# Hybrid block on one core: value transposes issued behind the inversion's recursion, gate projections ahead of query and key projections, long GpSimd operations cut in four

## The chip, the cores and the metric

The kernel runs on one core of a Trainium2 chip. The metric is the device time of one execution in microseconds (us), taken as the median of several. A core has five engines that work side by side and meet through semaphores: TensorE (PE in the profile, with PEld for its weight loads) does matmuls, VectorE (DVE) and ScalarE (ACT) do elementwise work, GpSimd (POOL) does elementwise work from on-chip memory to on-chip memory, and SyncE (SP) issues DMA transfers. [...]

## The reference

One encoder layer on 512 tokens of width 1024, all in float32. A single projection of the normalised input feeds a bidirectional RWKV-7 recurrence (8 heads of 64), a 2D neighbourhood attention (8 heads of 64) and 2048 gate logits. Both results are gated and projected back, and a mixture of experts follows (32 experts, two per token).

```python
h = rmsnorm(x, norm1_g)
p = h @ w_in
p_rwkv, q, k, v, gate_logits = jnp.split(p, IN_SPLITS, axis=-1)
y_a = rwkv7_bidirectional(p_rwkv, ...) @ w_o_rwkv
y_b = neighbourhood_attention_2d(q, k, v, q_gain, k_gain, rpb) @ w_o_na
g_a, g_b = jnp.split(jax.nn.sigmoid(gate_logits + b_gate), 2, axis=-1)
x = x + (g_a * y_a + g_b * y_b) @ w_out
x = x + hierarchical_moe(rmsnorm(x, norm2_g), ...)
```

The recurrence is, for each direction, head and token: `sa = S @ (-kk)`, then `S = S * w + outer(sa, kk * a) + outer(v, k)`, then `y = S @ r`. Inside the attention, q and k are normalised per head (a mean of squares, a reciprocal root, a gain) before they are used; v and the gates are not.

## The kernel before

Features lie on the 128 partitions and tokens along the free axis, so one "column block" of the projection is a tile of 128 x 512. A column block costs 24 matmuls 128x512, since each float32 product is made of three (high and low parts of the weights `w_hi`, `w_lo` and of the input `hT_hi`, `hT_lo`). ACT makes `w_hi`, and DVE or, for the late blocks, POOL makes `w_lo` (POOL in four parts of 128x256).

The recurrence is computed in chunks of 32 tokens, 16 chunks (`NCH`), for two groups of four heads (g = 0 and 1; a group has two column blocks q of two heads each). Each group goes through four stages:

- `prep(g)`: shifted inputs `sh_k`, `sh_r`, `sh_v`, the decays (`s`, `ep`), the scaled keys `KB`, and per chunk the matrices `T` (products `tp<-T,KB` on PE, masked by DVE into `T` or copied by ACT into `MT`).
- `invert(g)` (line 584): a triangular 32x32 matrix per chunk is inverted. DVE transposes `MT` into `NT`, runs a recursion of 15 steps on 16x16 halves (each one product `pr<-NT,TI` and one sum `TI<-TI,pr`, each depending on the last), and transposes the result twice (`MT<-TI`, `NT<-TI`, lines 609 and 611). Then PE multiplies by the off-diagonal part, once per direction d: `c<-MT,O`, ACT copies to `Q`, `c<-Q,NT`, and DVE adds to `MT`.
- `v_chunks(q)` (line 570): 16 DVE transposes 32x512 per group put the values into the state tile `R`. The first chain step reads them. `bonus_pair` (line 557) then makes `bv` on DVE and writes it to memory.
- `chain(g)` (chain_step, line 635): 16 steps, one after the other. A step is PE `c<-R,T`, ACT `X<-c`, PE `c<-X,MT`, ACT and DVE copies `R<-c`, PE `c<-R,T`, and two DVE sums `R<-c,EX` that start the next step. `chain_out` normalises the result.

PE has more to do beside this: `others(n)` (line 766) projects the next n of 28 further column blocks at a low priority, so that their matmuls fill PE's gaps. Block m = 0 to 3 is q, 4 to 7 is k (both end in `na_qk`, line 783), 8 to 11 is v (`na_v`), 12 to 27 are the gates. `na_qk` needs two ACT passes, eight small matmuls `x<-cst,osq` for the head sums, nine DVE operations on 128x8 (`ngx`, `nrs_i`, `nst`: a reciprocal root by Newton steps), a DVE copy `osq<-nst`, four matmuls `x<-cst,osq` 128x128, and the DVE products `oth<-oth,qg,x` (q) or `oth<-oth,pv,x` (k). A gate block needs one ACT tanh. All results are stored to memory and are read back by the attention (`na_inputs`, one half of the heads at a time) or by the gating. The blocks are taken 3, 5, 8 and 2 at a time (`OTH`), around `prep(0)`, `chain(0)` and `prep(1)`; then one after each of the eight attention blocks, which run beside `chain(1)`; then the rest.

The order of each engine's queue is fixed when the program is built: a list scheduler places instructions by priority as their operands come ready in its own model. So a change of source order or of priorities moves instructions on all engines.

Setting up at the start, `rwkv_consts` (lines 355 to 371) lets POOL copy identity blocks into the whole of `T` (four copies of 64x2048) and clear parts of `R` (four of 32x2048). In `prep_unit`, for the second direction, POOL adds the keys of both directions (`kd<-kd,kd`, 128x512, line 478), which `bonus_pair` reads.

After the attention follow the gating and output projection, the routing, and the experts, whose weights are streamed from memory.

## Time and profile before

| | us |
|---|---|
| median of three executions | 918.54 |
| lowest and highest of them | 910.8 and 920.9 |
| the profiled execution | 916.96 |
| its span, first to last instruction | 915.2 |

The profiled execution is read in these stages (us from the start of the span, as the first and last instructions of a stage stand in the timeline): set-up and first projections 0 to 40, prep 0 from 40 to 124.5, recursion 0 to 136.2, products of inversion 0 and first chain step to 166, chain 0 to about 264 with prep 1 begun beside it, prep 1 to 348.8, recursion 1 to 359.7, products and first chain step to 384, chain 1 and the attention to 513, remaining projections to 551, then gating, routing and experts to 915.

A row of a table by stretches gives start and end, the length, then the busy microseconds of PE, PEld, DVE, ACT and POOL (number of instructions in brackets), the granted TensorE clock as a share of full speed, the DMA share and GB/s. A row of a timeline gives start, length, engine, line, operation, result<-inputs, shapes, and in square brackets how long the engine had been idle and what ended that. A row of a table by groups ends with the count, the busy time in total, the mean of one in ns, and the idle time before them.

### The profile page before, as it was taken

How to read it: one execution, taken by the hardware profiler on the slowest of the kernel's cores; microseconds unless marked ns; L12 is line 12 of the kernel's file. 1: busy time of each engine (PE TensorE's matmuls, PEld its weight loads, DVE VectorE, ACT ScalarE, POOL GpSimd, SP SyncE). 2: the span in 40 equal slices, each digit the busy share in tenths (PEclk: the TensorE clock that was granted, in tenths of full speed). 3: DMA queues.
4: the chain of work that ended last, by engine and by line, in shares of the span. 5: the costliest groups of instructions: out<-in, count | busy, mean ns of one | idle time of the engine just before them, and what ended most of it. 6: DMA issues, size and time to landing. Idle time of an engine off the chain costs nothing. (4 is left out here: it accounts for less than half of the span.)

```text
span 915.2 us, 17391 instructions
## 1 busy us (share of the span) xinstructions
PE 809.7 (88%) x7192; PEld 526.2 (57%) x7192; DVE 419.5 (46%) x870; ACT 309.4 (34%) x667; POOL 199.4 (22%) x248
## 2 busy tenths in 40 slices
PE   8999886989988987799998999999579999888884
PEld 7776655656667665566666677878433333333331
DVE  5699883565788677124346205643612111111010
ACT  6544521222444553126647522223211111111110
POOL 2611231120004243132313430003411212211010
PEclk9999995999999998699999999999779999999998
DMA  6320130221112322321314648889889999999982
GB/s 220 114 73 33 36 103 27 70 72 66 46 62 87 101 70 71 131 91 44 116 45 138 189 134 317 300 316 401 343 358 411 389 362 398 394 394 399 399 339 44
DMA packets 49263, 176.18 MB, mean 193 GB/s; under 512 B 7584, under 2 KB 14368, under 8 KB 37152
## 3 DMA queue, kind: packets, MB, share of 16 engines
q1 hardware_dynamic: 43936, 164.56, 48.9%
q0 software_dynamic: 5248, 10.50, 4.3%
q8 instruction: 57, 0.93, 0.4%
q14 instruction: 22, 0.18, 0.1%
HBM read 159.30 MB, written 24.12 MB: 200 GB/s over the span
## 5 line engine op out<-in xcount | busy, mean ns | idle before, releaser
L191 POOL TENSOR_TENSOR w_lo<-w_raw,w_hi 128x256 fp32r<-128x256 f32 x116 | 88.7, 796 | 225.0 <-ACT w_hi L188 225.0
L203 PE MATMUL G<-ws,xT 128*64 128x512 f32 x512 | 128.8, 600 | 4.1 <-DMA ws<-in_wgu 2.8
L203 PE MATMUL mm<-hT_hi,w_lo 128*128 128x512 f32 x264 | 113.0, 428 | 8.4 <-ACT oth L188 7.6
L203 PE MATMUL mm<-hT_hi,w_hi 128*128 128x512 f32 x264 | 111.4, 422 | 0.0
L203 PE MATMUL mm<-hT_lo,w_hi 128*128 128x512 f32 x264 | 110.8, 420 | 0.0
L203 PEld LDWEIGHTS G<-ws,xT 128*64 128x64 f32 x512 | 44.5, 138 | 76.6 <-issue 65.4
L203 PE MATMUL Yd<-ws,hT 128*64 128x512 f32 x256 | 65.7, 606 | 9.7 <-ACT y L188 8.6
L188 ACT ACTIVATE w_hi<-w_raw 128x1024 fp32r<-128x1024 f32 x59 | 62.3, 1055 | 31.2 <-PE mm L203 31.2
L203 PEld LDWEIGHTS mm<-hT_hi,w_lo 128*128 128x128 f32 x264 | 51.4, 195 | 26.0 <-issue 15.5
L191 DVE TENSOR_TENSOR w_lo<-w_raw,w_hi 128x1024 fp32r<-128x1024 f32 x30 | 39.3, 1308 | 50.2 <-ACT w_hi L188 50.2
L203 PEld LDWEIGHTS mm<-hT_lo,w_hi 128*128 128x128 f32 x264 | 51.5, 195 | 12.7 <-issue 2.2
L203 PEld LDWEIGHTS mm<-hT_hi,w_hi 128*128 128x128 f32 x264 | 51.8, 196 | 11.3 <-issue 1.5
L1386 POOL DMA_INDIRECT out<-y,idx x16 | 25.2, 1577 | 117.1 <-DVE y L198 100.4
L191 DVE TENSOR_TENSOR sg<-sg,G 128x256 f32<-128x256 f32 x16 | 6.7, 420 | 95.9 <-ACT sg L188 95.9
L188 ACT ACTIVATE sg<-G,wts 128x256 f32<-128x256 f32 x16 | 7.6, 474 | 116.9 <-PE G L203 116.9
L198 DVE TENSOR_SCALAR y<-Yd,wts 128x512 f32<-128x512 f32 (+1 forms) x16 | 11.7, 734 | 77.1 <-PE Yd L203 62.6
L655 DVE COPY R<-c 32x128 f32<-32x128 f32 x64 | 18.8, 293 | 52.1 <-ACT R L188 51.4
L203 PEld LDWEIGHTS Yd<-ws,hT 128*64 128x64 f32 x256 | 16.6, 136 | 43.5 <-ACT y L188 21.6
L203 PE MATMUL c<-R,T 128*32 128x64 f32 (+1 forms) x992 | 36.5, 231 | 3.6 <-DVE R L191 1.3
L203 PE MATMUL tp<-T,KB 64*64 64x128 f32 x512 | 34.5, 278 | 5.6 <-ACT T L188 5.3
L203 PEld LDWEIGHTS c<-R,T 128*32 128x32 f32 (+1 forms) x992 | 26.2, 125 | 22.6 <-issue 10.5
L188 ACT ACTIVATE T<-tp 64x256 f32<-64x256 f32 x64 | 23.9, 378 | 42.8 <-DVE T L191 41.8
(313 smaller groups left out, 1454.3 us busy)
## 6 DMA issues: line engine op xcount, KB each, us to landing
ws<-in_wgu SPq DMA_DIRECT2D x64, 1024.0 KB, 21.0
ws<-in_wd SPq DMA_DIRECT2D x30, 1024.0 KB, 22.2
w_raw<-in_w_in SPq DMA_DIRECT2D x43, 512.0 KB, 3.6
d_oth<-oth SPq DMA_DIRECT2D x16, 256.0 KB, 3.1
w_raw<-in_wo SPq DMA_DIRECT2D x8, 512.0 KB, 3.8
w_raw<-in_w_out SPq DMA_DIRECT2D x8, 512.0 KB, 5.1
x_in<-in_x SPq DMA_DIRECT2D x4, 512.0 KB
ga<-d_oth SPq DMA_DIRECT2D x8, 256.0 KB, 4.5
```

Source lines behind the costliest of these rows:

```text
L188: self.nc.scalar.activation(out, in_, func, **kw)
L191: (eng or self.nc.vector).tensor_tensor(out, a, b, op=op)
L198: self.nc.vector.tensor_scalar(out, a, s1, None, op0=op0)
L203: return self.nc.tensor.matmul(out, l, r, start=start, stop=stop, **kw)
L655: self.nc.vector.tensor_copy(R[u, :, blk, p2], ps[u, 2:4])
L1386: self.nc.gpsimd.indirect_dma_start(out=self.A["out"], out_offset=bass.IndirectOffsetOnAxis(ap=idx, axis=0), in_=y, in_offset=None, bounds ...
```

## The change

Three things are changed.

1. The order in which `others` takes its blocks. It was 0, 1, 2, ... 27. It is now `TURN`: eight gates (12 to 19), then 0, 1, 4, 5, 8, 9, 2, 3, then 10, 11, then 6, 7 and 20 to 25 at the attention blocks, and 26, 27.
2. `v_chunks` may be issued only behind the last transpose of `invert` (`issue_after` holds the instructions of its body back until that one is issued; it isn't a wait on the chip).
3. Three kinds of POOL operations are made of four parts each: the copies into `T` (64x2048 to 64x512), the clearing of `R` (32x2048 to 32x512), and the sum `kd` (128x512 to 128x128).

```diff
+TURN = list(range(12, 20)) + [0, 1, 4, 5, 8, 9, 2, 3, 10, 11, 6, 7] + list(range(20, 28))
...
-                nc.gpsimd.tensor_copy(self.T[sr, :, d, blk, :, 64:], id64[sr, None, None].to_broadcast([64, NCH, 2, 64]))
+                for n in range(0, NCH, 4):
+                    nc.gpsimd.tensor_copy(self.T[sr, n:n + 4, d, blk, :, 64:], id64[sr, None, None].to_broadcast([64, 4, 2, 64]))
...
-            nc.gpsimd.memset(self.R[o:o + 32, :, :, blk, p2], 0.0)
+            for n in range(0, NCH, 4):
+                nc.gpsimd.memset(self.R[o:o + 32, n:n + 4, :, blk, p2], 0.0)
...
-            self.tt(self.kd[q], self.kd[q], kd, OP.add, eng=nc.gpsimd)
+            for o in range(0, T, P):
+                self.tt(self.kd[q][:, o:o + P], self.kd[q][:, o:o + P], kd[:, o:o + P], OP.add, eng=nc.gpsimd)
...
-        self.invert(g)
-        for q in (q0, q1):
-            self.v_chunks(q)
+        last = self.invert(g)
+
+        with self.tc.issue_after(last.ins):
+            for q in (q0, q1):
+                self.v_chunks(q)
         self.bonus_pair(q1)
...
-        nc.vector.transpose(out=D.rearrange("p u t -> p t u"), in_=TI.rearrange("p a b -> p b a"))
+        last = nc.vector.transpose(out=D.rearrange("p u t -> p t u"), in_=TI.rearrange("p a b -> p b a"))
...
             m = MT[:, d * NCH:(d + 1) * NCH]
             self.tt(m, m, ps, OP.add)
+        return last
...
-        for m in range(self.done, min(self.done + n, 28)):
+        for m in TURN[self.done:self.done + n]:
             ps = self.proj(15 + m, LOW)
```

In what follows, lines of the new kernel are 3 to 9 higher than those of the old (the transposes of the values are L581 before and L589 now). First, VectorE's queue at the end of recursion 0 and the start of chain 0. Before, it reads:

```order
L191 TENSOR_TENSOR TI<-TI,pr 128x2x15
L609 STREAM_TRANSPOSE MT<-TI 128x32x32
L194 SCALAR_TENSOR_TENSOR oth<-oth,qg,x 128x128 x4
L611 STREAM_TRANSPOSE NT<-TI 128x32x32
L191 TENSOR_TENSOR MT<-MT,c_1405 128x512
L191 TENSOR_TENSOR bv<-sh_v_989,tp 128x512
L191 TENSOR_TENSOR MT<-MT,c_1538 128x512
L200 TENSOR_SCALAR ngx<-x 128x8
L689 TENSOR_SCALAR nrs_i<-ngx 128x8
L200 TENSOR_SCALAR nst<-nrs_i 128x8
L191 TENSOR_TENSOR nrs_i<-nst 128x8
```

The same place now:

```order
L194 TENSOR_TENSOR TI<-TI,pr 128x2x15
L617 STREAM_TRANSPOSE MT<-TI 128x32x32
L619 STREAM_TRANSPOSE NT<-TI 128x32x32
L589 STREAM_TRANSPOSE R<-sh_v_473 32x16x32 x7
L194 TENSOR_TENSOR MT<-MT,c_1336 128x512
L589 STREAM_TRANSPOSE R<-sh_v_473 32x16x32
L589 STREAM_TRANSPOSE R<-sh_v_1019 32x16x32 x5
L194 TENSOR_TENSOR MT<-MT,c_1469 128x512
L589 STREAM_TRANSPOSE R<-sh_v_1019 32x16x32 x3
L194 TENSOR_TENSOR bv<-sh_v_1019,tp 128x512
L664 COPY R<-c_2470 32x2x64 x2
L194 TENSOR_TENSOR R<-c_2470,EX 64x2x128 x2
```

Thirteen of the sixteen value transposes now stand ahead of the second sum into `MT` and three behind it, with `bv` behind these and ahead of the first step's copies; the query's normalisation (`ngx`, `nrs_i`, `nst`) that stood ahead of the first step's copies is gone. Around inversion 1 the rows are the same as these.

Second, VectorE's queue in prep 1, where the second direction's keys are masked. Before:

```order
L191 TENSOR_TENSOR T<-tp,cst_107 64x4x64
L191 TENSOR_TENSOR T<-sh_r_2110,ep 64x16x32
L191 TENSOR_TENSOR kd<-kd,sh_k_2075 128x512
L194 SCALAR_TENSOR_TENSOR a<-a,kk 128x512
L191 TENSOR_TENSOR KB<-kd,s 128x16x32
L191 TENSOR_TENSOR KB<-a,s 128x16x32
L191 TENSOR_TENSOR T<-tp,cst_107 64x4x64 x2
L194 SCALAR_TENSOR_TENSOR T<-sh_k_2075,nkk,ep 64x16x31
```

The same place now:

```order
L197 SCALAR_TENSOR_TENSOR a<-a,kk 128x512
L194 TENSOR_TENSOR KB<-kd,s 128x16x32
L203 TENSOR_SCALAR ngx<-x 128x8
L194 TENSOR_TENSOR KB<-a,s 128x16x32
L698 TENSOR_SCALAR nrs_i<-ngx 128x8
L194 TENSOR_TENSOR T<-tp,cst_107 64x4x64
L203 TENSOR_SCALAR nst<-nrs_i 128x8
L194 TENSOR_TENSOR T<-tp,cst_107 64x4x64
L194 TENSOR_TENSOR nrs_i<-nst 128x8
L197 SCALAR_TENSOR_TENSOR T<-sh_k_1853,nkk,ep 64x16x31
```

The normalisations of blocks 0, 1 and 4 now stand between the operations of prep 1; that of block 5 stands in the same way between the 30 operations of recursion 1, those of 2 and 3 in chain 1 (steps 2 and 3), and those of 6 and 7 later in chain 1, between attention blocks. Before, block 0 stood in prep 0, block 1 in recursion 0, and blocks 2 to 7 in chain 0.

Third, TensorE's queue at the products of inversion 0 and the first chain step. Before:

```order
L203 MATMUL c_1471<-MT,O 32x32 x41
L203 MATMUL c_2516<-R,T 32x64 x8
L203 MATMUL mm<-hT_hi,w_lo 128x512
L203 MATMUL mm<-hT_hi,w_hi 128x512
L203 MATMUL c_1538<-Q,NT 32x32 x64
L203 MATMUL c_2516<-X,MT 32x64 x4
```

Now:

```order
L206 MATMUL mm<-hT_hi,w_lo 128x512
L206 MATMUL c_1469<-Q,NT 32x32 x64
L206 MATMUL c_2470<-R,T 32x64 x4
L206 MATMUL mm<-hT_hi,w_hi 128x512
L206 MATMUL mm<-hT_lo,w_hi 128x512
```

The first step's `c<-R,T`, which reads the transposed values, stood ahead of the last product `c<-Q,NT`; it now stands behind it, in two halves (the first is shown) with nine matmuls of a gate projection between them.

## The prediction

> **What bounds the kernel now.** I read the spans first, then the busy time of the engines over the whole, then by stretches, then the timelines of the engines inside the stretches that the change touches.

> ```profile
> core 0: 915.2 us, clock 0.956
> DMA  6320130221112322321314648889889999999982
> ```

> The profiled execution has 915.2 us between its first and last instruction and 1.8 around it (916.96). Each digit of the second row is a fortieth of the span, 22.9 us: memory traffic is light until about 550 us and then near full until the end. What the change touches lies before that. Whatever it saves or costs there shifts the loaded part as a whole, at full value.

> ```profile
> 40.00:124.50 84.50, 78.86 (x715) 54.82 (x714) 74.96 (x130) 41.92 (x79) 16.40 (x20) 0.96 0.19 57
> 124.50:136.20 11.70, 8.50 (x42) 6.40 (x41) 10.44 (x45) 2.50 (x4) 3.11 (x4) 1.00 0.33 112
> 140.00:160.00 20.00, 14.12 (x419) 11.24 (x420) 5.78 (x12) 3.35 (x7) 2.79 (x4) 0.54 0.08 29
> 166.00:221.00 55.00, 49.54 (x590) 33.57 (x590) 31.55 (x100) 17.75 (x43) 8.43 (x12) 0.99 0.17 59
> 300.00:348.80 48.80, 44.67 (x484) 31.97 (x485) 34.74 (x61) 26.37 (x60) 17.15 (x17) 1.00 0.21 61
> 348.80:359.70 10.90, 8.24 (x34) 5.87 (x33) 9.84 (x32) 3.66 (x5) 3.96 (x6) 1.00 0.29 97
> 360.00:380.00 20.00, 12.72 (x551) 10.12 (x552) 5.37 (x5) 1.53 (x4) 4.33 (x11) 0.51 0.50 163
> 384.00:412.00 28.00, 26.62 (x328) 17.63 (x316) 7.15 (x20) 8.93 (x22) 8.43 (x12) 1.00 0.27 86
> ```

> Prep 0 (first row) is loaded on both engines: PE 78.86 of 84.5 us, DVE 74.96. Prep 1 (fifth row) has DVE at 34.74 of 48.8, so room of 14 us, but PE at 44.67, room of 4.1. The recursions (second and sixth) are DVE's. Around the products of the inversions (third and seventh) PE and DVE both stand idle in turn and the clock is about half. In chain 0 with normalisations beside it (fourth) PE is idle 5.5 of 55 us; in chain 1 with gates beside it (last) 1.4 of 28. Two conclusions: PE is near its limit almost everywhere, so DVE time taken out is worth only the PE gaps that it closes; and the total of PE's work is unchanged, so any gain must be idle or half-clock PE time that goes away.

> **The change part by part.** All terms are against the profiled 916.96.

> *GpSimd's parts.* Its long operations, and what DVE paid beside them:

> ```profile
> L367 POOL COPY T<-id 64x2048 f32<-64x2048 f32 x4 | 8.5, 2141 | 0.1
> L191 POOL TENSOR_TENSOR kd<-kd,kd 128x512 f32<-128x512 f32 x4 | 8.7, 2176 | 60.1 <-DVE kd L191 60.1
> 28.54 2.91 DVE L191 TENSOR_TENSOR w_lo<-w_raw,w_hi 128x1024 fp32r<-128x1024 f32 x1
> 33.98 1.22 DVE L191 TENSOR_TENSOR w_lo<-w_raw,w_hi 128x1024 fp32r<-128x1024 f32 x1
> 98.96 1.78 DVE L191 TENSOR_TENSOR KB<-kd,s 128x512 f32<-128x512 f32 x1
> 100.67 0.68 DVE L191 TENSOR_TENSOR KB<-a,s 128x512 f32<-128x512 f32 x1
> ```

> One `w_lo` took 1.69 us longer than the next while POOL copied, one `KB` 1.10 longer than its neighbour while POOL summed. A quarter of either POOL operation is about 0.54 us, an estimate from the two means, so one DVE operation can be held by that instead. Ends: 0, if the next DVE operation is held by the next part, and -1.2 for the copies plus -0.6 for each of the two sums in prep 0, -2.4. I take -1, since nothing shows that DVE rather than PE ends the set-up. The clearing of `R` is hidden beside projections and costs nothing; if each new instruction had a cost, POOL's idle 60 us ahead of `kd` would cover it. [...]

> *Prep 0.* Sixteen value transposes and one normalisation leave it.

> ```profile
> L581 DVE STREAM_TRANSPOSE R<-sh_v x32: 692/702/708, 66.5 to 294.5; 32x512 f32<-32x512 f32 x32
> L191 DVE TENSOR_TENSOR nrs_i<-nst x24: 150/166/702, 116.3 to 224.3; 128x8 f32<-128x8 f32 x24
> L194 DVE SCALAR_TENSOR_TENSOR nrs_i<-nrs_i,ngx x24: 152/166/695, 117.5 to 224.5; 128x8 f32<-128x8 f32 x24
> L200 DVE TENSOR_SCALAR nst<-nrs_i x8: 172/558/721, 115.0 to 220.6; 128x8 int32<-128x8 int32 x8
> L414 DVE COPY osq<-nst 128x512 f32<-128x512 f32 x8 | 3.4, 428 | 0.4
> L194 DVE SCALAR_TENSOR_TENSOR oth<-oth,qg,x 128x128 f32<-128x128 f32 x16 | 4.4, 336 | 2.5 <-PE x L206 2.5
> 168.52 1.05 PE L203 MATMUL x<-cst,osq 128*128 128x2 f32 x8
> 174.68 0.63 PE L206 MATMUL x<-cst,osq 128*128 128x128 f32 x4 [0.31 <-DVE osq L414]
> ```

> Off DVE go 16 x 0.702 = 11.2 us, and for the normalisation 9 x 0.166 for the Newton operations (the third of them, `nst<-nrs_i,nst`, and the two at the start taken alike) + 0.56 + 0.17 + 0.43 + 4 x 0.336 = 4.0: 15.2 together. Off PE go only 1.05 + 0.63 = 1.7 us; the projection itself is replaced by a gate's. But PE is idle only 84.5 - 78.86 = 5.6 us here and loses (1 - 0.96) x 84.5 = 3.4 us to the clock. Ends: 0 (PE-bound) and -10.7 (all of the 5.6, 3.4 and 1.7). I take -5, the middle, since from 60 to 80 us PE has no gap to close:

> ```profile
> 60.00:80.00 20.00, 20.00 (x249) 14.74 (x247) 17.75 (x31) 8.78 (x18) 1.51 (x3) 1.00 0.23 71
> ```

> *Recursion 0.* It loses block 1's normalisation, and POOL's `w_lo` may still lengthen it:

> ```profile
> 128.23 0.29 DVE L191 TENSOR_TENSOR TI<-TI,pr 128x126 f32<-128x126 f32 x1
> 129.92 0.85 DVE L191 TENSOR_TENSOR pr<-NT,TI 128x126 f32<-128x126 f32 x1
> 136.19 2.00 DVE L609 STREAM_TRANSPOSE MT<-TI 128x1024 f32<-128x1024 f32 x1
> 138.05 1.04 DVE L194 SCALAR_TENSOR_TENSOR oth<-oth,qg,x 128x128 f32<-128x128 f32 x4
> 146.43 0.69 DVE L191 TENSOR_TENSOR MT<-MT,c 128x512 f32<-128x512 f32 x1 [5.36 <-PE c L203]
> 147.03 0.68 DVE L191 TENSOR_TENSOR bv<-sh_v,tp 128x512 f32<-128x512 f32 x1
> 153.54 0.69 DVE L191 TENSOR_TENSOR MT<-MT,c 128x512 f32<-128x512 f32 x1 [5.82 <-PE c L203]
> 361.43 1.97 DVE L611 STREAM_TRANSPOSE NT<-TI 128x1024 f32<-128x1024 f32 x1
> 380.24 0.30 DVE L655 COPY R<-c 32x128 f32<-32x128 f32 x1 [2.20 <-ACT R L188]
> ```

> It took 11.7 us, recursion 1 without a normalisation 10.9. Ends: -0.8 and, if the four POOL operations beside it (second row of the stretches) no longer hold one DVE operation each by 0.56 (0.85 against 0.29), another -2.2: -3.0. I take -1.5, nearer the recursion that was measured.

> *Products and first step.* Thirteen transposes (9.1 us) go into DVE's idle 5.36 + 5.82 = 11.2 us, which covers them; the order puts seven (4.9 us) ahead of the first sum and six (4.2) ahead of the second, and each set fits its gap. The last three and `bv` (2.1 + 0.7 = 2.8 us) stand ahead of the first step's copies, where group 1 shows 2.20 us of idle: up to +0.6, and the first `c<-R,T` now needs them. Against that, the product `oth` (1.04) between the two transposes goes, and the normalisation that delayed the first copies.

> ```profile
> 165.99 0.28 ACT L188 ACTIVATE X<-c 128x128 f32<-128x128 f32 x1 [5.17 <-PE c L203]
> 220.72 0.28 ACT L188 ACTIVATE X<-c 128x128 f32<-128x128 f32 x1 [0.24 <-PE c L203]
> 384.33 0.28 ACT L188 ACTIVATE X<-c 128x128 f32<-128x128 f32 x1 [3.50 <-PE c L203]
> 411.81 0.28 ACT L188 ACTIVATE X<-c 128x128 f32<-128x128 f32 x1 [3.08 <-PE c L203]
> 291.15 0.66 PE L206 MATMUL c<-cst,yc 128*128 128x128 f32 x4 [1.98 <-POOL yc L191]
> ```

> From `MT<-TI` to the second `X` group 0 took 165.99 - 136.19 = 29.8 us. In group 1 the second transpose starts at 361.43, so the first, 2 us long, at about 359.5: 24.8 us. Ends in group 0: -5.0 + 0.6 and +2.8 (the three transposes and `bv` in full, and nothing gained). I take -4.4, and in group 1 +0.6.

> *Chain 0.* From 165.99 to 220.72 are nine steps of 6.08 us with normalisations beside them; in chain 1, with gates, five steps from 384.33 to 411.81 take 5.50. 9 x 0.58 = -5.2. Ends: 0 and -5.5 - 5 x 1.7 = -14 (all idle PE time and all head sums gone). I take -5.2, the like for like.

> *Chain_out 0 and prep 1.* Its own value transposes leave; PE waits 1.98 us for the normalised result that they delayed. Ends 0 and -11.2; I take -1. Three normalisations come in: 12 us of DVE work into 14 us of room, 5 us of PE work into 4.1. Ends 0 and +12; I take +4, since PE's room is short by 1 and each normalisation makes PE wait for DVE once (0.31 in the row above; more where DVE is loaded). *Recursion 1* gets one: 0 to +4; I take +1, as recursion 0 with one was 0.8 longer. *Chain 1 and the attention* get four: 4 steps x 0.58 = +2.3 where two lie in steps, and 2 x 1.7 = +3.4 of PE work, partly into gaps; 0 to +11; I take +4.

> Sum: -1 - 5 - 1.5 - 4.4 + 0.6 - 5.2 - 1 + 4 + 1 + 4 = -8.5. 916.96 - 8.5 = 908.5, 10 us under the median of 918.54. A difference of about 1% (9.2 us) is what a measurement here can tell from no change.

> **The rivals.** *The work only moves (no change).* Prep 0 gives 0, for PE's 78.86 of 84.5 speaks for it; what chain 0 gains (-5.2) chain 1 and prep 1 pay back: -1 - 1.5 - 4.4 + 0.6 - 5.2 - 1 + 4 + 2 + 7 = +0.5, 917 to 918. The idle gaps of the third stretch speak against it.

> *Slower: the normalisations were free where they were, and aren't in prep 1.* There DVE would have 34.74 + 12 = 47 of 48.8 us, so every masked `T` and every `pr` start comes behind it. Prep 1 +12, recursion 1 +4, chain 1 +11, prep 0 0, the rest as above: -1 - 1.5 - 4.4 + 0.6 - 5.2 - 1 + 27 = +14.5, 931. It decides from the point where prep 1 and what follows cost over 22 us. DVE's room of 14 us speaks against it.

> *Twice as much.* Prep 0 gives its whole 10.7, chain 0 8, prep 1 and later cost 4 in all: -2 - 10.7 - 1.5 - 4.4 - 8 - 1 + 4 = -23.6, 893. A part of it could come from the clock: 14.12 us of PE at 0.54 in the products would save 6.5 at full speed, if the fillers kept PE busier there. Group 1 had no normalisation in its recursion and still shows 0.51, so I give this 1 in 20, within this rival. [...]

> **How the numbers follow.** Forecast (900 to 913) 0.46; work only moves (913 to 925) 0.23; slower (925 to 936) 0.16; twice as much (887 to 900) 0.15. The time is the forecast's, 908.5. The range leaves out the slower case and the lower third of the largest gain, about 2 in 10: 893 to 926. Faster by over 1% is below 909.4: all of 0.15 and two thirds of 0.46, 0.46. Slower by over 1% is above 927.7: 0.14. Within: 0.40.

> **What would show it.** In the profile after: value transposes between 137 and 155 us and no DVE idle over 3 us there; `pr` starting 5 us earlier than 124.5; the `X` of chain 0 about 5.5 us apart; first `T` mask to `pr` of group 1 4 us longer; chain 1 started about 10 us earlier than 384. If `pr` starts no earlier, prep 0 was PE's; if chain 1 starts at 384 or later, prep 1 paid for it all. I am wrong if the attention waits for blocks 6 and 7, which now come late, or if the first step waits for the last transposes.

## The result, and the profile after

The changed kernel takes 903.07 us (median of four executions, 900.11 to 909.27) against 917.31 before; the ratio is 0.985, with a 95% interval of 0.980 to 0.990. So it is faster by 14 us (1.5%), where 10 were forecast (908.5, range 893 to 926). The profiled execution after has this row in the table of spans; before it was 915.2 us at 0.956:

```profile
core 0: 902.6 us, clock 0.965
```

Where the time went is seen best stage by stage, each from its first to its last event. The table by stretches of the kernel before (length, then busy PE, PEld, DVE, ACT, POOL with their instructions, granted clock, DMA share, GB/s), for prep 0, the products of inversion 0 with the first chain step, the rest of chain 0, from there to the first mask of prep 1, prep 1, the products of inversion 1, the rest of chain 1, and from there to the gating:

```profile
70.37:124.55 54.18, 50.22 (x469) 34.10 (x470) 48.12 (x91) 28.80 (x58) 12.59 (x17) 0.94 0.14 45
...
136.19:165.99 29.80, 22.82 (x618) 17.31 (x617) 13.24 (x30) 4.04 (x8) 2.79 (x4) 0.66 0.15 47
165.99:261.63 95.64, 89.06 (x1031) 60.64 (x1030) 61.38 (x158) 33.17 (x76) 10.09 (x15) 0.98 0.18 59
261.63:306.48 44.85, 39.33 (x484) 31.08 (x480) 35.20 (x64) 18.22 (x46) 13.44 (x17) 0.96 0.32 98
306.48:348.84 42.36, 38.42 (x439) 26.94 (x436) 31.07 (x55) 24.17 (x55) 13.91 (x13) 1.00 0.18 55
...
359.65:384.33 24.68, 17.05 (x594) 13.18 (x595) 7.15 (x9) 2.01 (x5) 4.68 (x11) 0.59 0.40 132
384.33:472.70 88.37, 86.17 (x1075) 59.45 (x1074) 34.26 (x89) 47.77 (x144) 25.78 (x52) 1.00 0.25 76
472.70:550.98 78.28, 69.46 (x520) 52.05 (x514) 26.56 (x52) 39.92 (x94) 26.11 (x37) 1.00 0.47 146
```

The same stages of the changed kernel:

```profile
71.24:116.51 45.27, 44.07 (x450) 29.29 (x447) 33.18 (x59) 27.90 (x57) 15.08 (x20) 1.00 0.13 39
...
126.86:150.12 23.26, 16.74 (x603) 12.85 (x604) 18.29 (x25) 3.65 (x8) 2.81 (x4) 0.78 0.20 69
150.12:230.35 80.23, 78.82 (x949) 52.41 (x948) 40.60 (x85) 31.08 (x70) 11.33 (x18) 1.00 0.22 71
230.35:266.36 36.01, 31.29 (x482) 25.20 (x477) 27.43 (x58) 16.05 (x39) 11.21 (x13) 1.00 0.31 102
266.36:316.03 49.67, 46.44 (x463) 33.45 (x462) 38.32 (x91) 24.30 (x51) 12.71 (x16) 0.90 0.13 45
...
328.90:355.79 26.89, 21.23 (x622) 16.11 (x623) 18.46 (x25) 5.80 (x15) 6.57 (x11) 0.81 0.27 85
355.79:450.14 94.35, 87.85 (x1059) 60.97 (x1058) 46.35 (x136) 38.13 (x111) 24.43 (x46) 0.98 0.26 78
450.14:534.95 84.81, 79.10 (x599) 58.53 (x593) 30.70 (x67) 52.21 (x137) 29.54 (x49) 1.00 0.49 153
```

The first four stages got shorter by 8.9, 6.5, 15.4 and 8.8 us, and the first mask of prep 1 came 40 us earlier (266.36 against 306.48). The next four got longer by 7.3, 2.2, 6.0 and 6.5, and recursion 1 between them by 2.1; when the gating starts, 16 us are left (534.95 against 550.98), and at the end of the span 12.6. The change moved 40 us and kept a third of it. Two things are worth reading in the rows. TensorE's busy time falls with the length in every stage that got shorter, so it is not only its waiting that went: it did less work there, or did it faster, and some of that work is found again later (79.10 us busy in the last row instead of 69.46). And the clock in the products rose from 0.66 and 0.59 to 0.78 and 0.81.

At the inversion VectorE now works where it waited. Its timeline after: the start of the recursion (124.55 before), the transposes around the two sums, and the first step's copy.

```profile
116.51 0.19 DVE L194 TENSOR_TENSOR pr<-NT,TI 128x30 f32<-128x30 f32 x1 [3.50 <-PE tp L206]
...
130.47 4.94 DVE L589 STREAM_TRANSPOSE R<-sh_v 32x512 f32<-32x512 f32 x7
135.42 0.69 DVE L194 TENSOR_TENSOR MT<-MT,c 128x512 f32<-128x512 f32 x1
136.12 4.31 DVE L589 STREAM_TRANSPOSE R<-sh_v 32x512 f32<-32x512 f32 x6
141.19 0.69 DVE L194 TENSOR_TENSOR MT<-MT,c 128x512 f32<-128x512 f32 x1 [0.76 <-PE c L206]
141.89 2.14 DVE L589 STREAM_TRANSPOSE R<-sh_v 32x512 f32<-32x512 f32 x3
144.06 0.69 DVE L194 TENSOR_TENSOR bv<-sh_v,tp 128x512 f32<-128x512 f32 x1
146.44 0.30 DVE L664 COPY R<-c 32x128 f32<-32x128 f32 x1 [1.69 <-ACT R L191]
```

The thirteen transposes fill the two gaps that were 5.36 and 5.82 us, and the last three with `bv` still leave 1.69 us of idle time ahead of the copy. The recursion itself now waits 3.50 us for TensorE: VectorE is early. The first step does stand behind the last transposes: the second half of its `c<-R,T` starts at 144.73, 0.7 us after they end, and the first `X` comes 18.3 us after the first transpose behind the recursion (13.3 before). The second `X` then follows after 5.0 us. Before it took 16.5, with the second sum and block 2's normalisation in between (at 157 us, so in this stage and not in chain 0).

### The profile page after: what moved, and what is told of

Its sections match the earlier page's. It is cut to its first block, busy times and chain, and to the rows that moved or that the text cites. A ratio compares the mean times of both kernels' runs of the same rounds, so it can differ in the third digit from the quotient of the medians.

```text
span 902.6 us, 17431 instructions
## 1 busy us (share of the span) xinstructions
PE 805.1 (89%) x7192; PEld 522.0 (58%) x7192; DVE 413.6 (46%) x870; ACT 309.6 (34%) x667; POOL 206.6 (23%) x284
## 5 line engine op out<-in xcount | busy, mean ns | idle before, releaser
L206 PE MATMUL G<-ws,xT 128*64 128x512 f32 x512 | 129.7, 601 | 5.8 <-DMA ws<-in_wgu 4.4
L194 POOL TENSOR_TENSOR w_lo<-w_raw,w_hi 128x256 fp32r<-128x256 f32 x116 | 88.3, 792 | 188.5 <-ACT w_hi L191 178.8
L206 PE MATMUL mm<-hT_hi,w_lo 128*128 128x512 f32 x264 | 111.9, 424 | 4.8 <-ACT oth L191 2.8
L206 PE MATMUL mm<-hT_hi,w_hi 128*128 128x512 f32 x264 | 110.3, 418 | 0.0
L206 PE MATMUL mm<-hT_lo,w_hi 128*128 128x512 f32 x264 | 109.8, 416 | 0.0
L206 PEld LDWEIGHTS G<-ws,xT 128*64 128x64 f32 x512 | 44.9, 138 | 78.8 <-issue 64.7
L206 PE MATMUL Yd<-ws,hT 128*64 128x512 f32 x256 | 65.7, 606 | 9.7 <-ACT y L191 8.7
L191 ACT ACTIVATE w_hi<-w_raw 128x1024 fp32r<-128x1024 f32 x59 | 62.3, 1055 | 30.4 <-PE mm L206 30.4
L206 PEld LDWEIGHTS mm<-hT_hi,w_lo 128*128 128x128 f32 x264 | 50.6, 192 | 19.8 <-issue 7.0
L206 PEld LDWEIGHTS mm<-hT_hi,w_hi 128*128 128x128 f32 x264 | 50.6, 192 | 11.5 <-issue 2.3
L206 PEld LDWEIGHTS mm<-hT_lo,w_hi 128*128 128x128 f32 x264 | 50.6, 192 | 11.6 <-issue 1.3
L194 DVE TENSOR_TENSOR w_lo<-w_raw,w_hi 128x1024 fp32r<-128x1024 f32 x30 | 37.3, 1242 | 37.2 <-ACT w_hi L191 37.2
L194 DVE TENSOR_TENSOR sg<-sg,G 128x256 f32<-128x256 f32 x16 | 6.7, 421 | 97.9 <-ACT sg L191 97.9
L191 ACT ACTIVATE sg<-G,wts 128x256 f32<-128x256 f32 x16 | 7.6, 475 | 119.5 <-PE G L206 119.5
L201 DVE TENSOR_SCALAR y<-Yd,wts 128x512 f32<-128x512 f32 (+1 forms) x16 | 11.7, 734 | 77.5 <-PE Yd L206 63.0
L206 PEld LDWEIGHTS Yd<-ws,hT 128*64 128x64 f32 x256 | 16.6, 136 | 43.5 <-ACT y L191 21.6
L206 PEld LDWEIGHTS c<-R,T 128*32 128x32 f32 (+1 forms) x992 | 26.5, 124 | 24.6 <-DVE R L664 11.3
L191 ACT ACTIVATE T<-tp 64x256 f32<-64x256 f32 x64 | 24.0, 377 | 46.4 <-DVE T L194 45.4
L206 PE MATMUL c<-R,T 128*32 128x64 f32 (+1 forms) x992 | 36.8, 229 | 2.7 <-DVE R L194 1.6
L206 PE MATMUL tp<-T,KB 64*64 64x128 f32 x512 | 36.1, 287 | 2.8 <-ACT T L191 2.6
```

The lines of the kernel that those rows point to most:

```text
L191: self.nc.scalar.activation(out, in_, func, **kw)
L194: (eng or self.nc.vector).tensor_tensor(out, a, b, op=op)
L201: self.nc.vector.tensor_scalar(out, a, s1, None, op0=op0)
L206: return self.nc.tensor.matmul(out, l, r, start=start, stop=stop, **kw)
```

## The experiments

Each time below is a median, and each ratio is against the kernel before on the same chip, with its 95% interval. "Stage" means the stages of the tables above.

**The three parts alone.** The first kernel has only the late transposes, the second only the new order, the third only the divided GpSimd operations, the fourth the first two.

```diff
+        last = self.invert(g)
...
+        with self.tc.issue_after(last.ins):
+            for q in (q0, q1):
+                self.v_chunks(q)
...
```

> The kernel before with the value transposes behind the inversion's recursion, and nothing else of the change. Theory: the transposes are what shortened prep 0 and the way from the end of chain 0 to prep 1, so the first recursion starts 6 to 8 us earlier than 124.5, the first mask of prep 1 comes 12 to 18 us earlier than 306.5, and the products of both inversions get 1 to 3 us longer; the whole is 8 to 13 us shorter than before. Rival: TensorE bounds prep 0 and it was the query's normalisation that made it wait; then the first recursion starts within 2 us of 124.5 and the whole is within 4 us of before.

901.34 us, ratio 0.985 (0.979 to 0.991).

```diff
+TURN = list(range(12, 20)) + [0, 1, 4, 5, 8, 9, 2, 3, 10, 11, 6, 7] + list(range(20, 28))
...
-        for m in range(self.done, min(self.done + n, 28)):
+        for m in TURN[self.done:self.done + n]:
```

> The kernel before with the new order of the further projections, and nothing else. Theory: chain 0 gets shorter by about 10 us (nine steps from the second on at 4.9 instead of 6.1 us) and the products of inversion 0 by 4 to 6, the first recursion starts within 3 us of 124.5; in prep 1 and later 12 to 17 us are paid back; the whole is 0 to 5 us shorter than before. Rival (the order is the whole change): 12 to 15 us shorter. Rival (the order only pays with the transposes out of the way): slower than before by 3 us or more.

915.42 us, ratio 1.002 (0.999 to 1.005).

```diff
-                nc.gpsimd.tensor_copy(self.T[sr, :, d, blk, :, 64:], id64[sr, None, None].to_broadcast([64, NCH, 2, 64]))
+                for n in range(0, NCH, 4):
+                    nc.gpsimd.tensor_copy(self.T[sr, n:n + 4, d, blk, :, 64:], id64[sr, None, None].to_broadcast([64, 4, 2, 64]))
...
-            self.tt(self.kd[q], self.kd[q], kd, OP.add, eng=nc.gpsimd)
+            for o in range(0, T, P):
+                self.tt(self.kd[q][:, o:o + P], self.kd[q][:, o:o + P], kd[:, o:o + P], OP.add, eng=nc.gpsimd)
```

> The kernel before with GpSimd's copies, clears and key sums in four parts, and nothing else. Theory: single VectorE operations beside them are held for less long, but the stages do not end there; the whole is within 2 us of before, and prep 0 starts and ends within 1.5 us of where it did. Rival: the hold of up to 2 us per long operation lies on the path; 3 to 5 us shorter.

914.85 us, ratio 1.000 (0.997 to 1.003).

```diff
+TURN = list(range(12, 20)) + [0, 1, 4, 5, 8, 9, 2, 3, 10, 11, 6, 7] + list(range(20, 28))
...
+        with self.tc.issue_after(last.ins):
...
```

> The new order and the late value transposes together, with GpSimd's operations whole as before. Theory: within 2 us of the changed kernel (903), since the parts add nothing. Rival: the parts carry 3 us or more of the gain, 906 or more.

901.69 us, ratio 0.987 (0.981 to 0.993).

The late transposes are the whole gain. The divided GpSimd operations and the new order bring nothing that these intervals show, alone or with the transposes. The divided operations did shorten what they were to shorten: the `w_lo` that took 2.91 us beside the long copy now takes 1.22, and the two `KB` of prep 0 beside the sum `kd` take 1.90 together instead of 2.46. But these rows don't lie on the path, for the first mask of prep 0 came no earlier (72.5 us against 70.4).

```profile
28.85 1.22 DVE L191 TENSOR_TENSOR w_lo<-w_raw,w_hi 128x1024 fp32r<-128x1024 f32 x1
```

In detail the theory of the late transposes held only in part. With the transposes alone the first recursion starts at 120.29, 4.3 us earlier (6 to 8 expected); the first mask of prep 1 comes 13.9 earlier, as expected. The products of inversion 0 got 2.1 longer, those of inversion 1 not (24.07). In inversion 0 the first step did wait for the last transposes here, which end at 155.59:

```profile
155.65 0.32 PE L203 MATMUL c<-R,T 128*32 128x64 f32 x8 [1.68 <-DVE R L583]
```

The milestones of these kernels are, in us from the start of the span:

| | before | order alone | transposes alone | both (changed kernel) |
|---|---|---|---|---|
| recursion 0 starts | 124.55 | 123.37 | 120.29 | 116.51 |
| second `X` of chain 0 | 165.99 | 154.36 | 165.42 | 150.12 |
| last `X` of chain 0 | 261.63 | 236.91 | 258.52 | 230.35 |
| first mask of prep 1 | 306.48 | 284.16 | 292.64 | 266.36 |
| second `X` of chain 1 | 384.33 | 380.68 | 370.53 | 355.79 |
| last `X` of chain 1 | 472.70 | 473.76 | 454.16 | 450.14 |
| gating starts | 550.98 | 549.64 | 536.49 | 534.95 |

The order alone is 24.7 us ahead at the end of chain 0, and 1.1 behind at the end of chain 1; none of the 0 to 5 us that were expected of it is seen. Its rows for the products of inversion 0, those of inversion 1, and the rest of chain 1:

```profile
133.71:154.36 20.65, 15.15 (x595) 12.00 (x596) 7.14 (x9) 3.65 (x7) 2.81 (x4) 0.68 0.10 33
...
347.24:380.68 33.44, 23.28 (x612) 18.10 (x613) 13.03 (x26) 4.04 (x9) 5.46 (x12) 0.59 0.34 110
380.68:473.76 93.08, 88.75 (x1063) 61.73 (x1062) 43.02 (x125) 44.66 (x130) 25.43 (x48) 0.98 0.22 68
```

The products of inversion 0 got 9.1 us shorter, those of inversion 1 8.8 longer. What happened there is what had stood at inversion 0 before: VectorE's timeline of this kernel shows a query's normalisation between the second sum and the first step's copy.

```profile
365.52 0.69 DVE L192 TENSOR_TENSOR MT<-MT,c 128x512 f32<-128x512 f32 x1 [6.92 <-PE c L204]
369.44 0.17 DVE L201 TENSOR_SCALAR ngx<-x 128x8 f32<-128x8 f32 x1 [3.23 <-PE x L204]
...
373.42 0.30 DVE L656 COPY R<-c 32x128 f32<-32x128 f32 x1
```

The order moved the normalisations. That their price went with them, and that this is why the order brings nothing, is read from such rows and not shown.

**Which group's transposes.** The late transposes in one group alone.

```diff
+        if g == 0:
+            with self.tc.issue_after(last.ins):
+                for q in (q0, q1):
+                    self.v_chunks(q)
+        else:
+            for q in (q0, q1):
+                self.v_chunks(q)
...
```

> The kernel before with the late value transposes in group 0 alone. Theory: prep 0 gets 4 us shorter, the products of inversion 0 give 2 to 4 of it back, and the whole is 1 to 4 us shorter than before (about 3 of the 14). Rival (the gain is prep 0's, and carries through): 8 us or more shorter.

909.45 us, ratio 0.994 (0.993 to 0.996).

```diff
+        if g == 1:
...
```

> The kernel before with the late value transposes in group 1 alone. Theory: the way from the last step of chain 0 to the first mask of prep 1 gets shorter by 9 to 11 us of 44.9, products 1 stay within 1 us of 24.7 as TensorE does projections in the gaps of its own, and the whole is 9 to 12 us shorter than before. Rival (both groups alike, since both lose 11.2 us of VectorE work): 6 to 8 us shorter.

905.18 us, ratio 0.990 (0.987 to 0.993).

Group 1 carries about two thirds (-1.0%) and group 0 a third (-0.6%, 6.4 us by the medians, more than the 4 expected); together they make the -1.5% of both. In group 1 eleven of the sixteen transposes stood inside the normalisation of chain 0's result, a chain of dependent small VectorE operations. The timeline of the kernel before shows its first and last row:

```profile
278.49 0.16 DVE L689 TENSOR_SCALAR rs_i<-gx 128x16 int32<-128x16 int32 x1
...
290.74 0.90 DVE L191 TENSOR_TENSOR yc<-yc,gst 128x512 f32<-128x512 f32 x1
```

and the one with late transposes in group 1:

```profile
275.15 0.15 DVE L696 TENSOR_SCALAR rs_i<-gx 128x16 int32<-128x16 int32 x1
...
278.84 0.69 DVE L191 TENSOR_TENSOR yc<-yc,gst 128x512 f32<-128x512 f32 x1
```

12.25 us became 3.69. The stage from the last `X` of chain 0 to the first mask of prep 1 took 33.95 us instead of 44.85, and 8.6 of these 10.9 us are the chain's.

```profile
258.81:292.76 33.95, 29.64 (x446) 23.43 (x439) 25.04 (x47) 16.16 (x41) 11.39 (x13) 1.00 0.31 102
```

This kernel also says how far one execution can be trusted in prep 0, where its instructions are those of the kernel before (469 matmuls, 91 VectorE operations in both): the stage took 51.71 us at a clock of 1.00, not 54.18 at 0.94. Of the 4.3 us that the late transposes seemed to save in prep 0 (49.87 us), 2.5 are this difference in clock, and 1.8 are left.

```profile
70.55:122.26 51.71, 47.71 (x469) 32.15 (x470) 47.93 (x91) 28.65 (x58) 12.52 (x17) 1.00 0.15 47
```

**Is it TensorE's time that counts?** In the kernel with late transposes, work is taken from TensorE, beside chain 0 and behind the attention (four blocks each are projected without the low parts of weights and input).

```diff
             for k in range(8):
+                if m - 15 in range(4, 8):
+                    self.mm(ps, hi[:, k], hh[:, k], start=(k == 0), stop=(k == 7))
+                    continue
```

> The kernel with late value transposes in both groups (901.3), and four key projections that run beside chain 0 made of one product instead of three: 64 matmuls 128x512 less on TensorE, 14.6 us at 0.228 each; the low parts of weights and input are left out for these four blocks. Theory (TensorE's time is the currency up to the gating, wherever it is saved): 11 to 15 us shorter than without the cut, 886 to 891, since later projections move forward into the place and the last ones end earlier. Rival (chain 0 is bound by its own steps and the projections only fill gaps): within 4 us of 901.

897.74 us, ratio 0.983 (0.978 to 0.988).

```diff
+                if m - 15 in range(24, 28):
...
```

> The same cut in the last four gate projections, which run behind the attention; the low parts are left out for these four blocks. Theory: 13 to 15 us shorter than without the cut, 886 to 889, as in the run with the cut in chain 0. Rival (the streamed expert weights hide it): within 4 us of 901.

892.72 us, ratio 0.977 (0.973 to 0.981).

In the profiled executions the cut in chain 0 brought the gating forward by 10.1 us (526.43 against 536.49), the cut in the tail by 11.5 (525.04). That speaks for TensorE's time as the currency wherever it is saved. But an estimated 14.6 us of matmuls were left out (64 at 0.228 each; 24 of them in a row start 0.227 us apart in the kernel before, from 48.53 to 53.74), and the medians fell by only 3.6 and 8.6. Neither theory's range was met, and for chain 0 the median lies within the 4 us of the rival, so these runs don't decide the question there. The rows of the first for chain 0 and for the tail show how the work moved, chain 0 even longer than before:

```profile
162.65:267.09 104.44, 94.08 (x1028) 65.06 (x1027) 66.63 (x165) 38.49 (x85) 18.63 (x27) 0.95 0.25 79
...
468.77:526.43 57.66, 45.95 (x399) 36.51 (x391) 19.87 (x37) 21.56 (x44) 18.37 (x25) 0.97 0.54 171
```

What is missing went two ways. TensorE's idle time ahead of the gating rose from 45.7 to 52.8 us, 10.4 of it in chain 0 (6.0 without the cut). And the clock fell, to 0.95 in chain 0 (0.98 without the cut); its mean over the span was 0.962 and 0.958 in the two executions of 893.5 and 894.7 us, and 0.952 and 0.951 in the two of about 901.

**Are the normalisations what makes the order worthless?** The Newton operations are taken out of the kernel with late transposes, with the old order and with the new.

```diff
-        for _ in range(3):
+        for _ in range(0 if name == "nrs_i" else 3):
```

> The kernel with late value transposes and the old order of projections; the nine Newton operations 128x8 of each of the eight query and key normalisations are left out (the first guess of the root is used). Theory: TensorE's idle time in chain 0 (6.0 of 93.1 us with them) falls below 3, and the whole is 2 to 6 us shorter than 901. Rival (the normalisations cost nothing where they stand): within 2 us.

906.93 us, ratio 0.992 (0.989 to 0.995).

> The kernel with late value transposes and the new order, and the same nine operations left out. Theory (a normalisation makes TensorE wait for about as long wherever it stands, and the new order only moves these waits from chain 0 to prep 1, recursion 1 and chain 1): the new order and the old stay within 4 us of each other without these operations too, and TensorE's idle time in chain 1 (6.7 of 95.9 us with them) falls below 4. Rival (the new order would pay, but for normalisations that are dearer in prep 1 and chain 1): 6 us or more shorter than the old order without them.

905.59 us, ratio 0.989 (0.984 to 0.995).

The two orders stay together (1.3 us apart, 0.4 with the operations), as the theory has it, and the rival that the new order would pay without them falls. But both kernels took longer with less to do: 5.6 us over the kernel with late transposes, whose interval just touches, and 3.9 over the one with both, where 2 to 6 less were expected. Chain 0 with the old order, and chain 1 with the new:

```profile
159.88:266.27 106.39, 98.98 (x1035) 67.77 (x1034) 56.27 (x117) 34.84 (x78) 10.94 (x15) 0.92 0.20 61
```

```profile
351.82:447.10 95.28, 91.62 (x1016) 62.88 (x1015) 33.98 (x94) 34.39 (x99) 24.17 (x42) 0.89 0.24 72
```

TensorE's idle time didn't fall below 3 in chain 0 (7.4 us of 106.4, more projections in it), and did fall below 4 in chain 1 (3.7); both have a clock of about 0.9. The scheduler set another order for all engines in these kernels too, so the loss belongs to the removal and the new order together. Prep 1, where the new order puts normalisations, took 47.9 us without their Newton operations (at a clock of 0.93) and 46.6 with them (at 1.00). So these runs don't show that the normalisations are what makes the order worthless; why it is stays open.

**Another order.** Four gates first, then all query and key blocks.

```diff
-TURN = list(range(12, 20)) + [0, 1, 4, 5, 8, 9, 2, 3, 10, 11, 6, 7] + list(range(20, 28))
+TURN = [12, 13, 14, 15, 0, 4, 1, 5, 2, 3, 6, 7, 8, 9, 10, 11] + list(range(16, 28))
```

> The changed kernel with another order: four gates first, then all query and key projections, so that their normalisations stand in chain 0 and none in prep 0, recursion 0, or the products of inversion 0. Theory: the products of inversion 0 get as short as in the changed kernel (23 us from the first transpose to the second step) and chain 1 as short as with the old order (84 us), and the whole is 1 to 5 us shorter than 902. Rival (the order doesn't matter to the whole, as projections only change places): within 1 us of 902, or slower.

900.74 us, ratio 0.983 (0.979 to 0.987). The normalisations did not all go where they were meant to: four start in chain 0 (at 164, 177, 190 and 202 us), the others at 272, 293 and 310, around and in prep 1, and at 330 in recursion 1. So the run is another mixture and no test of a prep 1 without normalisations. The products of inversion 0 are short (23.4 us) as expected, and chain 1 is nearly so (87.0 from its second `X`, 84 expected); prep 1, recursion 1 and the products of inversion 1 took 47.8, 13.7 and 28.8 us, against 43.5, 10.3 and 24.1 with the old order. The whole is 0.6 to 2.3 us below the kernels with late transposes and other orders, which the intervals can't tell apart.

**Keeping TensorE busy.** Additional matmuls in the kernel with late transposes, where TensorE waits for the inversion's transposes.

```diff
+        keep = self.bank("Y0", [P, T], 1)
+        for i in range(5):
+            self.mm(keep, f(TI)[:, :P], f(TI)[:, T:])
         nc.vector.transpose(out=MT.rearrange("p u t -> p t u"), in_=TI)
```

> The kernel with late value transposes and the old order, and ten additional matmuls of 128x512 whose results nobody reads: five per group, on TensorE while it waits 2.8 and 3.0 us for VectorE's two transposes behind the recursion (about 2.5 us each time). Theory (that wait is what takes the clock down to half in the products): the half-clock stretches of 11 and 14 us at 136 and 348 us shrink to 7 us or less each, the mean granted clock rises from 0.967 to 0.970 or more, and the whole is 2 to 6 us shorter than 901, below every other order. Rival (the small products themselves, 32x32, take the clock down): the stretches stay within one step of 3.4 us, the clock within 0.002, and the whole is 0 to 3 us longer.

927.24 us, ratio 1.012 (1.009 to 1.016): slower, outside both expectations. The added matmuls took almost twice what was reckoned (4.56 us instead of 2.5); each of the five stands in TensorE's timeline as two, ten in all:

```profile
133.73 4.56 PE L203 MATMUL Y<-TI 128*128 128x512 f32 x10 [2.22 <-DVE TI L191]
```

So the products began over 4 us late (6.5 us after the first transpose starts, 2.0 without them), the first sum of inversion 0 came 14.1 us after the first transpose instead of 10.2, and most of the loss lies elsewhere. In the profiled execution (the longest of six, 933.68), the stage from the last `X` of chain 1 to the gating took 100.2 us (82.3 without them), at a clock of 0.91.

```profile
464.00:564.16 100.16, 91.28 (x604) 66.88 (x599) 27.47 (x61) 48.71 (x121) 29.28 (x46) 0.91 0.41 128
```

Of these 17.9 us, 8.5 are half clock (17.1 us from 470 on), and 2.6 are idle time. The additions stand over 100 us ahead of this stage; that they act there through the order which the scheduler made of all that follows is likely and not shown. On the question itself: the time at half clock in the products, in steps of 1 us, fell from about 10 to 7 us at inversion 0 and from about 14 to 10 around inversion 1, one step of about 3.4 us each. With TensorE kept busy ahead of the small products the clock fell later (12.3 us after the first transpose instead of 2.7 at inversion 0), but still fell. That the waits alone take it down is not shown.

## Time and clock apart

The executions of one kernel differ, and they differ by their clock: over 79 executions of the thirteen kernels other than the one before, each taken against the mean of its kernel, 0.01 of mean granted clock goes with 6.5 us (correlation -0.85). The product of an execution's time and its clock has a standard deviation of 0.4 to 2.4 us only. So the product, "time at full clock", helps to tell work and waiting from clock:

| kernel | mean us | mean clock | time x clock, us |
|---|---|---|---|
| before (58 executions) | 914.8 | 0.959 | 877.4 |
| divided GpSimd operations | 914.9 | 0.959 | 877.5 |
| late transposes in group 0 | 909.6 | 0.964 | 876.8 |
| late transposes in group 1 | 904.7 | 0.963 | 871.0 |
| late transposes in both | 901.3 | 0.967 | 871.3 |
| order alone | 916.6 | 0.951 | 871.9 |
| order and late transposes | 902.5 | 0.966 | 871.6 |
| changed kernel | 903.9 | 0.964 | 870.9 |
| late transposes, no Newton operations | 907.4 | 0.958 | 869.2 |
| order and late transposes, no Newton operations | 906.5 | 0.961 | 870.7 |
| mixed order | 900.3 | 0.966 | 869.7 |
| less matmul work in chain 0 | 897.5 | 0.956 | 857.8 |
| less matmul work in the tail | 893.4 | 0.963 | 860.6 |
| added matmuls | 927.9 | 0.961 | 891.3 |

The product takes too much out, though. If all time went with the clock, 0.01 of clock would be worth 9.5 us, and 6.5 were measured, so a part of the time doesn't go with it. Therefore each saving is given twice here, by the product and, as an estimate, by the 6.5 us at equal clock; that the 6.5, measured within kernels, holds between them isn't shown. Late transposes in group 0 saved 0.6 or 2 of their 5 us, and the rest is clock. Those in group 1 saved 6.4 or 8 of 10, and in both groups 6 or 9 of 13.5. The order alone saved 5.5 or 3.4 and gave it back in clock, 0.951 against 0.959. Less work in chain 0 saved 13.5 or 11 of its 14.6 us, and lost 10 or 7 to the clock. The direction is the same both ways, the size is known to a few microseconds.

The clock falls in steps. The table by stretches of the kernel before, around the products of inversion 0 in steps of 2 us:

```profile
140.00:142.00 2.00, 0.00 (x0) 0.00 (x0) 1.07 (x1) 0.18 (x1) 0.00 (x0) 0.94 0.33 123
142.00:144.00 2.00, 1.82 (x127) 1.82 (x128) 0.00 (x0) 0.00 (x0) 0.00 (x0) 0.50 0.03 8
...
158.00:160.00 2.00, 2.00 (x7) 1.52 (x6) 1.82 (x6) 0.00 (x0) 1.37 (x2) 0.50 0.00 0
160.00:162.00 2.00, 1.96 (x12) 1.15 (x10) 1.68 (x7) 0.27 (x1) 0.00 (x0) 0.50 0.81 211
162.00:164.00 2.00, 2.00 (x20) 1.50 (x19) 1.12 (x4) 0.00 (x0) 0.00 (x0) 0.94 0.13 51
```

The clock is at half for about 20 us, also from 156 to 162, where TensorE is busy throughout, nearly all the time with 128x512 matmuls. Over the first 560 us of the kernel before, the stretches at half clock are 3.4 us long or whole multiples of it, and lose 27 us in all: 10.2 at each inversion, and 1.7 each at 104, 114, 220 and 292 us. With late transposes they lose 17: 5.1 and 6.8 at the inversions, where more projections stand between the products (35 of their matmuls instead of 27, and 30 instead of 18), and three single steps. These 10 us of one execution each are more than the 5 to 7 that the estimates above give to the clock; a part of them lies in time in which TensorE waited.

## Why the prediction was right, and where it wasn't

The time and its sign were right, and so was the first conclusion: that TensorE is near its limit and a gain can only be idle or half-clock TensorE time. Over the 551 us before the gating TensorE was busy 494.6 us; with late transposes it was busy 490.8 of 536.5, with the same 5729 matmuls. Idle time fell by 10.7 and busy time by 3.7; busy time holds the slow clock too (128x512 matmuls start 0.43 us apart at half clock, at 221 us of the kernel before, and 0.23 at full, at 224).

The sum was right by terms that were not, and that was luck. Its gains add up to -18.1 and what is paid back to +9.6; in the profile the gains are -41.0 and the payback is +24.1. Both were put at less than half, and the errors mostly cancelled. The payback is more than the 22 us from which the slower rival was to decide; it did not come because the gains were larger as well. (That 22 doesn't follow from the prediction's own terms: with prep 0 at nothing, as in this rival, the other terms add up to -12.5, and the change costs time from 12.5 on.) The signs that it named came true in direction: recursion 0 started 8.0 us earlier (5 forecast), the `X` of chain 0 stood 4.88 us apart (5.5), chain 1 started 28.5 earlier (10). Step by step, prediction against the changed kernel's profile:

- GpSimd's parts, -1: nothing (0 at full clock and in the ratio). The holds got shorter (1.22 us instead of 2.91) and lay off the path. The far end of the term, -2.4, took the time held for time on the path, and the runs show 0.
- Prep 0, -5: measured -8.9, of which the transposes alone give -4.3. The size fits by luck: TensorE's idle time rose there from 4.0 to 4.9 us, and 2.5 of the 4.3 are the clock (0.94 to 0.99), which this stage also got with its transposes where they had been (51.71 us at 1.00, above). The order alone gave -1.5, and some 3 of the 8.9 came only with both together.

```profile
70.42:120.29 49.87, 45.00 (x459) 30.57 (x456) 39.93 (x76) 27.74 (x56) 13.51 (x17) 0.99 0.16 48
```

- Recursion 0, -1.5: measured -1.3.
- Products, -4.4: measured -6.5. The order alone gives -9.1 and the transposes alone +2.1; the two parts of the term had been seen, with their signs. With the transposes alone the first step waits for the last of them (1.68 us of idle time), which the prediction had named as a sign of being wrong; in the changed kernel what left this stage counts for more.
- Chain 0, -5.2: measured -10.8 over the nine steps that the term covers, and -15.4 over all fourteen from the second `X` to the last; the other five had been put at nothing without a reason. In the nine a step took 4.88 us, while 5.50 had been taken from chain 1 as the mean of five steps between 4.93 and 6.74. The shortest would have been the better guide.

```profile
150.12 0.28 ACT L191 ACTIVATE X<-c 128x128 f32<-128x128 f32 x1 [3.08 <-PE c L206]
194.07 0.28 ACT L191 ACTIVATE X<-c 128x128 f32<-128x128 f32 x1 [1.07 <-PE c L206]
```

- Chain_out 0 and prep 1, -1 for the transposes: this is the step that failed. Measured -8.8, and in the kernel with group 1's transposes alone -10.9. The prediction took the 1.98 us that TensorE waited for the result as the worth of the whole chain. TensorE had been filled with projections during the rest of its 12 us, and that seemed to make the rest worthless. But projections can be done later, in gaps that stay: 111 of their matmuls stood in that stage before and 80 with group 1's transposes late, and 18 against 30 in the products of inversion 1. Here the chain got 8.6 us shorter, the stage 10.9 and the kernel 10.6, 6 to 8 of them at equal clock, where TensorE's wait had shown 1.98.
- Prep 1 +4, recursion 1 +1, products 1 +0.6, chain 1 and attention +4: measured +7.3, +2.1, +2.2 and +12.5. All were too low, by a factor of 2 to 4. They pay back what the order saved; the predicted terms of the order added up to a small gain, and no gain was measured.

So the gain was foretold mostly for the wrong part: about -3.5 for the transposes, -4 for the order and -1 for GpSimd (with prep 0's -5 shared out by the VectorE time of each), where -13.5, 0 and 0 were measured for each alone. The rival "the work only moves" is true of the order. The rival by which the products would get back their clock had been given 1 chance in 20, because group 1 without normalisations showed 0.51 as well. That row was read rightly and the conclusion drawn too far: it showed that the half clock comes without normalisations too, not that nothing in the change could shorten it. By the two estimates above the clock gave a third to a half of the gain of the late transposes.

That attention would wait for blocks 6 and 7 wasn't tried by itself; the stage behind chain 1 is 6.5 us longer in the changed kernel, with 79.1 us of TensorE work in it instead of 69.5 and 5.7 us of idle time instead of 8.8, so nothing asks for such a wait.

## What to carry to other kernels

Where an engine is filled with movable work, don't read the price of a dependent chain from that engine's wait: in this kernel the filler hid it and was done later, so measure the chain from its first to its last row and ask which gaps remain for the filler. Reordering that filler shortened some stages here by 25 us and lengthened later ones by 23. And look at the granted clock beside the time: here two edits with nearly the same product of time and clock (the order, and group 1's transposes) differed by 12 us, of which an estimated 7.5 go with the clock, and 14.6 us of work left out beside chain 0 bought 3.6.
